# Order of the gate rows and of the residual tiles in the feed-forward stages of a two-layer encoder trunk

## The chip, the cores and the metric

The kernel runs on one core of a Trainium2 chip. The metric is the device time of one execution in microseconds; lower is better. The engines are TensorE (PE in the profile, its weight loads PEld), VectorE (DVE), ScalarE (ACT), GpSimd (POOL) and SyncE (SP, which here only issues transfers). Each engine works through its own queue in order, and they wait for each other by semaphores.

## The reference

Two layers over 512 frames of 1024 features, float32. Layer 0 has latent attention, layer 1 chunked attention with a relative-position bias; each is followed by a SwiGLU feed-forward with 2816 hidden features, and each sub-layer is wrapped in two RMS norms.

```
def swiglu(h, w_gate, w_up, w_down):
    return (jax.nn.silu(h @ w_gate) * (h @ w_up)) @ w_down

for layer in range(2):
    h = rms_norm(x, attn_pre_g[layer])
    ...
    x = x + rms_norm(y, attn_post_g[layer])
    h = rms_norm(x, ffn_pre_g[layer])
    f = swiglu(h, ffn_w_gate[layer], ffn_w_up[layer], ffn_w_down[layer])
    x = x + rms_norm(f, ffn_post_g[layer])
```

## The kernel before

All float32 products are done as three matmuls of a reduced type: each operand is split into a high half (a cast on ScalarE, `whi<-raw`, line 144) and a low half (a subtraction on VectorE, `wlo<-raw,whi`, line 146), and high-high, high-low and low-high are summed in PSUM. Three buffers each hold the halves of a weight tile, so the cast of a tile waits until the product three before it has been done.

The feed-forward hidden features come in blocks of 128. The first two blocks of a layer are done whole and kept in SBUF (`kept`, the tiles `fu`); the other 20 are done in ten pairs by `products`, pair 0 to 9, with a scheme of Strassen's kind: seven products (j = 0 to 6) of half size in place of eight. Each product is 24 matmuls of 128x256 on TensorE: two output halves e = 0, 1 of 12 each. The PSUM banks are `be` (products 0 and 6), `al` (1, 3, 4, 5) and `ga` (2). Product 5 adds to the banks that product 4 has filled, so the VectorE addition that reads product 4 out (`ut<-al,ut`, line 1648) must be done before product 5 starts in the same bank. In words like "fifth product", the product with j = 4 is meant. Sums of weight tiles are made partly by VectorE (`raw<-raw,raw`, line 202) and partly by transfers of GpSimd's queue that add in memory (line 185).

The gate rows: when the RMS norm's factor is known, it is spread over a tile `bc` (line 524), each finished gate block is multiplied by it (`fu<-fu,bc`, line 1236, for the two whole blocks, `gt<-gt,bc`, line 1594, for the others), goes through SiLU on ScalarE (line 1237 or 1595, the first with a load of the activation table) and is multiplied with its up block to a hidden tile `hd`, from which four half-size sums `hs` are formed for the down product. These are closures in the list `units`; `products` calls one at products 1, 3 and 5 of a pair (in pair 1 at product 6).

In layer 1 a generator `by_tokens` also runs beside the pairs from pair 2 on. For each of the eight residual tiles it loads 128x512 from the buffer `mid` in memory (`x<-mid`, line 1275, on SyncE), turns it in blocks of 32x32 on VectorE (`xt<-x`, line 1278) and stores it to the output in four transfers (`out_x<-xt`, line 1281), where the feed-forward result is added later. It is resumed at five of the seven products.

The order on each engine is set by a list scheduler over the traced program: what is ready first and stands first in the program is queued first. `with behind(ins):` queues the instructions of the block that are on the engine of `ins` behind `ins`, in the queue's order only, without a wait.

Of the kernel before, what the change touches and what calls it, by code (L numbers as in the profile page):

```python
# [14 lines left out]
OP = mybir.AluOpType  # L15
# [4 lines left out]
KT = D // P  # L20
# [48 lines left out]
def trunk(ctx: ExitStack, tc: tile.TileContext, a, out):  # L69
    nc = tc.nc  # L70
    V = nc.vector
# [20 lines left out]
    def bank(tag="mm", name="b"):  # L92
        return ps.tile([P, S], F32, tag=tag, name=name_(name), bufs={"mm": 4, "s": 2, "t": 2}[tag])
# [62 lines left out]
    class Pair:  # L156
# [35 lines left out]
        def load(self, j):  # L192

            if j == 0:
                self.raw[5] = self.tile(3)
            elif j in (1, 2):
                self.raw[j] = self.tile(j - 1)
                return self.last
# [78 lines left out]
    class Feed:  # L277
# [96 lines left out]
        def next(self, n, ahead=True):  # L374
            i = self.pos
            self.pos += 1
            assert self.plan[i][1] == n
            self.split(i + int(ahead))
            return self.ready[i]
# [44 lines left out]
    def behind(ins):  # L424

        return tc.issue_after(ins.ins) if ins is not None else nullcontext()

    def cut(t, c):
        return t[0][:, c], t[1][:, c]
# [412 lines left out]
    x = []  # L842
# [309 lines left out]
    def ffn(i, x_src, osp, firsts, late=()):  # L1152
# [96 lines left out]
        def step_():  # L1249
            for n in (5, 6):  # L1250
                with behind(at["ut"]), behind(feed.low):
                    feed.lows[base + n] = at["t"] = next(more)[1]
                if n == 5:
# [6 lines left out]
                    for k, (p, j) in enumerate([(0, 5), *((1, j) for j in range(7))]))  # L1260
        units = [lambda f=f: gate(*kept[2 * f:2 * f + 2]) for f in range(N_WHOLE)]
        products(xs, tb, rb, hid, side, units, empty, at, by_tokens(H) if i else None)
        post = (AfterLast if i else After)(i, eps, H)
        down(hid, post)
# [5 lines left out]

    def by_tokens(make):

        for k in range(KT):
            x = make(name="x")
            nc.sync.dma_start(x, a["mid"][:, k])
            yield
            t = make(name="xt")
            V.transpose(t, x)
            yield
            for q in range(4):  # L1280
                nc.sync.dma_start(
                    bass.AP(tensor=out.tensor, offset=out.offset + k * P + 32 * q, ap=[[D, 32], [32 * D, S // 32], [1, 32]]),
                    t[32 * q:32 * q + 32].rearrange("i (b j) -> i b j", j=32))
            yield
# [84 lines left out]
    A0, A1 = HALF  # L1369
# [216 lines left out]
    def products(xs, tb, rb, hid, side, units, empty, at, aside=None):  # L1586

        K2 = KT // 2
        moving = [[cut(tb[k][0], A0) for k in range(K2)], [cut(xs[k], A0) for k in range(K2)],
                  [cut(xs[k + K2], A0) for k in range(K2)], [cut(tb[k][0], A1) for k in range(K2)],  # L1590
                  [cut(tb[k][1], A0) for k in range(K2)], [cut(tb[k][1], A1) for k in range(K2)],
                  [cut(xs[k + K2], A1) for k in range(K2)]]
        def gated(t, u):
            V.tensor_tensor(t, t, rb[0], op=OP.mult)
            nc.scalar.activation(t, t, AF.Silu)
            h = hid.room()
            V.tensor_tensor(h, t, u, op=OP.mult)
            hid.add(h)

        pairs = (NF - N_WHOLE) // 2  # L1600
        done = mm = None
        for p in range(pairs):
            al, ga = [], []
            be = [bank("t" if p % 2 else "s", "be") for _ in range(2)]
            make = U if p > 3 else hid.make
            gate = [make(name="gt") for _ in range(2)]
            up_ = [make(name="ut") for _ in range(2)]
            for j in (range(7) if p else FIRST_TURN):
                if (p, j) in side:
                    side[p, j]()  # L1610
                if p and j in ((6,) if p == 1 else (1, 3, 5)[:2 + (aside is None or p % 2 == 0)]) and units:
                    units.pop(0)()
                if aside is not None and p > 1 and j in (0, 1, 3, 5, 6):
                    next(aside, None)
                w = feed.next(1024, 2)
                done = mm if p < 3 else None
                if p + 1 == pairs and j >= 4:
                    hid.ahead(j // 5)
                if j == 1:
                    al = [bank(name="al") for _ in range(2)]  # L1620
                if j == 2:
                    ga = [bank(name="ga") for _ in range(2)]
                to = (be, al, ga, al, al, al, be)[j]
                for e in range(2):
                    o = to[e][:, A0]
                    for k in range(K2):
                        l, r = w(e * S + k * P, P), moving[j][k]
                        first_ = j < 3 and k == 0
                        with behind(done):
                            for n, (c, d) in enumerate(((0, 0), (0, 1), (1, 0))):  # L1630
                                mm = nc.tensor.matmul(o, l[c], r[d], start=first_ and n == 0, stop=k == K2 - 1 and n == 2,  # L1631
                                                      skip_group_check=True)
                    t, u = gate[e], up_[e]
                    if j == 0:
                        at["ut"] = nc.scalar.copy(u[:, A1], o)
                    elif j == 1:
                        with behind(None if p else empty):
                            nc.scalar.copy(t[:, A0], o)
                    elif j == 2:
                        if p:  # L1640
                            V.tensor_tensor(t[:, A0], t[:, A0], o, op=OP.add)
                    elif j == 3:
                        nc.scalar.copy(t[:, A1], o)
                        if not p:
                            with behind(at["t"]):
                                V.tensor_tensor(t[:, A0], t[:, A0], ga[e][:, A0], op=OP.add)
                    elif j == 4:
                        V.tensor_tensor(u[:, A1], o, u[:, A1], op=OP.add)  # L1648
                    elif j == 5:
                        nc.scalar.copy(u[:, A0], o)  # L1650
                    else:
                        V.tensor_tensor(t[:, A1], t[:, A1], o, op=OP.add)
                        units.append(lambda t=t, u=u: gated(t, u))
                        while p > 6 and units:
                            units.pop(0)()
# [14 lines left out]
    x, sx = post.x, post.split  # L1670
# [21 lines left out]
    at = feed.pos  # L1692
# [249 lines left out]
```

## Time and profile before

| | |
|---|---|
| median of 3 runs | 1103.87 us (1102.91 to 1104.52) |
| profiled execution | 1103.36 us, of which the profile's span is 1101.6 us |
| granted TensorE clock, mean | 0.997 |
| busy: TensorE, VectorE, ScalarE, GpSimd | 99%, 83%, 63%, 12% of the span |
| matmuls of the ten pairs (line 1631) | layer 0: from 212.0 us on, layer 1: up to 985 us |

Rows of a timeline read: start in us, length in us, engine, line, operation, output and inputs by tile names, shape, count, and in brackets the idle time of the engine before it with what ended it. A row with x2 holds two instructions in a row. The ends of matmuls are modelled, so that their lengths overlap. In the chain of waits each row is a start, a length and what the time went to.

### The profile page before, as it was taken

How to read it: one execution, taken by the hardware profiler on the slowest of the kernel's cores; microseconds unless marked ns; L12 is line 12 of the kernel's file. 1: busy time of each engine (PE TensorE's matmuls, PEld its weight loads, DVE VectorE, ACT ScalarE, POOL GpSimd, SP SyncE). 2: the span in 40 equal slices, each digit the busy share in tenths (PEclk: the TensorE clock that was granted, in tenths of full speed). 3: DMA queues.
4: the chain of work that ended last, by engine and by line, in shares of the span. 5: the costliest groups of instructions: out<-in, count | busy, mean ns of one | idle time of the engine just before them, and what ended most of it. 6: DMA issues, size and time to landing. Idle time of an engine off the chain costs nothing.

```text
span 1101.6 us, 19401 instructions
## 1 busy us (share of the span) xinstructions
PE 1088.5 (99%) x7037; PEld 983.7 (89%) x7037; DVE 913.3 (83%) x1661; ACT 693.9 (63%) x1355; POOL 127.2 (12%) x193
## 2 busy tenths in 40 slices
PE   9999999999999999999999999999999999999997
PEld 7887889999999998888888888889999999998885
DVE  7787747889988879978858898758899989789977
ACT  7576637866555556668636767657765555566675
POOL 2211100111000001500000110000110010002401
PEclk9999999999999999999999999999999999999999
DMA  7444217797777648961555677618898888749913
GB/s 241 120 116 136 69 39 257 202 263 186 173 196 187 178 148 269 161 192 49 192 152 163 155 203 186 171 59 276 202 263 187 250 206 225 201 161 266 168 30 76
DMA packets 91216, 191.99 MB, mean 174 GB/s; under 512 B 27136, under 2 KB 28928, under 8 KB 91120
## 3 DMA queue, kind: packets, MB, share of 16 engines
q1 hardware_dynamic: 75904, 151.29, 44.2%
q0 software_dynamic: 14784, 39.02, 20.0%
q8 instruction: 55, 0.90, 0.3%
q10 hardware_dynamic: 432, 0.44, 0.1%
q14 instruction: 41, 0.34, 0.1%
HBM read 157.26 MB, written 10.88 MB: 153 GB/s over the span
## 4 chain that ended last, share of the span: by engine, by line
PE 96%; DMA 1%; DVE 1%; issue 1%; ACT 1%; SPq 0%; DVEq 0%; POOLq 0%; POOL 0%; ACTq 0%
PE al L1631 20%; PE b L393 10%; PE b L394 10%; PE b L395 10%; PE be L1631 10%; PE al L1362 8%; PE be L1362 5%; PE ga L1631 5%; PE de L1362 3%; PE ga L1362 3%; PE pt L577 2%; PE b L1792 2%; PE b L1125 1%; PE sc L1784 1%; DMA x<-mid 1%; PE sc L1783 1%
## 5 line engine op out<-in xcount | busy, mean ns | idle before, releaser
L144 ACT CAST whi<-raw 128x1024 fp32r<-128x1024 f32 (+3 forms) x224 | 225.1, 1006 | 189.6 <-PE al L1631 64.5
L146 DVE TENSOR_TENSOR wlo<-raw,whi 128x1024 fp32r<-128x1024 f32 (+3 forms) x224 | 260.9, 1167 | 58.2 <-ACT whi L144 56.6
L1631 PE MATMUL al<-th,whi 128*128 128x256 f32 x464 | 132.6, 286 | 2.0 <-DVE ut L1648 2.0
L1631 PE MATMUL al<-tl,whi 128*128 128x256 f32 x464 | 130.0, 280 | 0.0
L1631 PE MATMUL al<-th,wlo 128*128 128x256 f32 x464 | 130.0, 280 | 0.0
L1631 PEld LDWEIGHTS al<-th,whi 128*128 128x128 f32 x464 | 87.3, 188 | 4.6 <-DVE ut L1648 2.6
L1631 PEld LDWEIGHTS al<-tl,whi 128*128 128x128 f32 x464 | 87.4, 188 | 0.0
L1631 PEld LDWEIGHTS al<-th,wlo 128*128 128x128 f32 x464 | 87.3, 188 | 0.0
L564 ACT ACTIVATE p<-p,mn 128x128 f32<-128x128 f32 (+1 forms) x96 | 54.1, 563 | 35.2 <-DVE mn L562 33.2
L146 DVE TENSOR_TENSOR ptl<-pt,pth 128x128 fp32r<-128x128 f32 (+1 forms) x96 | 46.6, 486 | 31.2 <-ACT pth L144 30.4
L393 PE MATMUL b<-xh,whi 128*128 128x512 f32 x170 | 71.7, 422 | 0.0
L185 POOL DMA_DIRECT2D raw<-in_w_pair x40 | 35.4, 885 | 297.4 <-DMA raw<-in_w_pair 81.5
L146 DVE TENSOR_TENSOR wlo<-wd,whi 128x512 fp32r<-128x512 f32 x86 | 56.3, 685 | 14.6 <-ACT whi L144 14.4
L394 PE MATMUL b<-xl,whi 128*128 128x512 f32 x170 | 66.7, 393 | 0.0
L395 PE MATMUL b<-xh,wlo 128*128 128x512 f32 x170 | 66.7, 392 | 0.0
L144 ACT CAST whi<-wd 128x512 fp32r<-128x512 f32 x86 | 49.8, 619 | 24.0 <-PE al L1362 10.7
L144 ACT CAST pth<-pt 128x128 fp32r<-128x128 f32 (+1 forms) x96 | 40.3, 422 | 32.3 <-PE pt L577 31.4
L1362 PE MATMUL al<-whi,pl 128*128 128x512 f32 x132 | 51.4, 390 | 0.0
L1362 PE MATMUL al<-whi,ph 128*128 128x512 f32 x132 | 51.4, 389 | 0.0
L1362 PE MATMUL al<-wlo,ph 128*128 128x512 f32 x132 | 51.4, 389 | 0.0
L1631 PE MATMUL ga<-xh,whi 128*128 128x256 f32 x160 | 45.0, 281 | 0.0
L1631 PE MATMUL al<-xh,whi 128*128 128x256 f32 x160 | 44.9, 280 | 0.0
(332 smaller groups left out, 3482.6 us busy)
## 6 DMA issues: line engine op xcount, KB each, us to landing
raw<-in_w_pair SPq DMA_DIRECT2D x104, 512.0 KB, 5.3
raw<-in_w_pair POOLq DMA_DIRECT2D x40, 512.0 KB, 7.7
wd<-in_w_down SPq DMA_DIRECT2D x54, 256.0 KB, 5.4
raw<-in_w_o SPq DMA_DIRECT2D x16, 512.0 KB, 3.8
raw<-in_w_down SPq DMA_DIRECT2D x16, 512.0 KB, 3.9
raw<-in_w_qkb SPq DMA_DIRECT2D x16, 512.0 KB, 3.6
wd<-in_w_down POOLq DMA_DIRECT2D x22, 256.0 KB, 5.1
wd<-raw POOLq DMA_DIRECT2D x22, 256.0 KB, 4.2
```

What stands on the lines that cost most here:

```text
L144: hi = nc.scalar.copy(dst_hi, src)
L146: return hi, V.tensor_tensor(dst_lo, src, dst_hi.bitcast(F32), op=OP.subtract)
L185: return nc.gpsimd.dma_start(self.raw[j], src, accum_op=OP.add)
L393: nc.tensor.matmul(o, l[0], r[0], start=start, stop=False)
L394: nc.tensor.matmul(o, l[0], r[1], start=False, stop=False)
L395: last_mm[0] = nc.tensor.matmul(o, l[1], r[0], start=False, stop=stop)
L564: nc.scalar.activation(p[:, :n], p[:, :n], AF.Exp, bias=mn[:, :1], scale=-1.0, accum_out=self.sums[:, qt:qt + 1])
L577: nc.tensor.transpose(t[:, kt * P:(kt + 1) * P], p[:, kt * P:(kt + 1) * P], ident)
L1125: nc.tensor.matmul(o[:, q_], va[kt][:, part, v_], pt[:, kt, q_], start=n + kt == 0, stop=n == 2 and kt == NQT - 1)
L1362: nc.tensor.matmul(to[e], l[c], r[d], start=j < 4 and k == 0 and n == 0, stop=k == NF // 2 - 1 and n == 2, skip_group_check=True)
L1631: mm = nc.tensor.matmul(o, l[c], r[d], start=first_ and n == 0, stop=k == K2 - 1 and n == 2, skip_group_check=True)
L1792: nc.tensor.matmul(o[:, q_], vv, pt[:, kt, q_], start=pt is pth and kt == 0, stop=pt is ptl and kt == NQT - 1)
```

## The change

First, the units that are called in pairs 0 to 2 (in effect pairs 1 and 2) are queued on VectorE behind the last addition of a fifth product (`at["last"]`, which the fifth product now sets). Second, `by_tokens` issues the load of tile k + 1 at the step in which it used to issue only the load of tile k, so one more tile is held.

```
     def by_tokens(make):
 
-        for k in range(KT):
+        def load(k):
             x = make(name="x")
             nc.sync.dma_start(x, a["mid"][:, k])
+            return x
+
+        next_ = load(0)
+        yield
+        for k in range(KT):
+            x, next_ = next_, load(k + 1) if k + 1 < KT else None
             yield
             t = make(name="xt")
             V.transpose(t, x)
...
                 if p and j in ((6,) if p == 1 else (1, 3, 5)[:2 + (aside is None or p % 2 == 0)]) and units:
-                    units.pop(0)()
+                    with behind(at["last"] if p < 3 else None):
+                        units.pop(0)()
...
                     elif j == 4:
-                        V.tensor_tensor(u[:, A1], o, u[:, A1], op=OP.add)
+                        at["last"] = V.tensor_tensor(u[:, A1], o, u[:, A1], op=OP.add)
```

The number of instructions and their order on TensorE and GpSimd stay as they are. In the changed kernel the lines behind the first piece are 6 higher, and those behind the second 7, so `ut` is line 1655 there and `xt` line 1284.

VectorE in layer 0, from the end of pair 1's fourth product to pair 2's first (the numbers after the names tell tiles apart: `ut_2927` and `ut_2928` are the two additions of pair 1's fifth product, `wlo_3087` belongs to its seventh product, `wlo_3118` and `wlo_3159` to pair 2's first and second). Before:

```order
L202 TENSOR_TENSOR raw_2529<-raw_2529,raw_2776 128x1024
L1236 TENSOR_TENSOR fu_2639<-fu_2639,bc_3082 128x512
L1236 TENSOR_TENSOR fu_2641<-fu_2641,bc_3082 128x512
L146 TENSOR_TENSOR wlo_3087<-raw_2529,whi_3086 128x1024
L1648 TENSOR_TENSOR ut_2927<-al_2971,ut_2927 128x256
L1648 TENSOR_TENSOR ut_2928<-al_2972,ut_2928 128x256
L1239 SCALAR_TENSOR_TENSOR hd_3150<-fu_2639,fu_2640 128x512
L1594 TENSOR_TENSOR gt_2666<-gt_2666,bc_3082 128x512
L146 TENSOR_TENSOR wlo_3118<-raw_2887,whi_3117 128x1024
```

After:

```order
L202 TENSOR_TENSOR raw_2529<-raw_2529,raw_2776 128x1024
L1655 TENSOR_TENSOR ut_2927<-al_2971,ut_2927 128x256
L146 TENSOR_TENSOR wlo_3087<-raw_2529,whi_3086 128x1024
L1655 TENSOR_TENSOR ut_2928<-al_2972,ut_2928 128x256
L1236 TENSOR_TENSOR fu_2639<-fu_2639,bc_3082 128x512
L146 TENSOR_TENSOR wlo_3118<-raw_2887,whi_3117 128x1024
L1236 TENSOR_TENSOR fu_2641<-fu_2641,bc_3082 128x512
L202 TENSOR_TENSOR raw_2887<-raw_2887,raw_3010 128x1024
L1239 SCALAR_TENSOR_TENSOR hd_3150<-fu_2639,fu_2640 128x512
L1659 TENSOR_TENSOR gt_2925<-gt_2925,be_2923 128x256
L146 TENSOR_TENSOR wlo_3159<-raw_3010,whi_3158 128x1024
```

The two `fu` multiplications have moved from ahead of the `ut` additions to behind them, and the `gt` multiplications further back. Layer 1 has the same move at the same place.

ScalarE at the same place of layer 0. Before:

```order
L144 CAST whi_3086<-raw_2529 128x1024
L1237 ACT_TABLE_LOAD
L1237 ACTIVATE fu_2639<-fu_2639 128x512
L144 CAST whi_3117<-raw_2887 128x1024
L1237 ACTIVATE fu_2641<-fu_2641 128x512
L1650 COPY ut_2927<-al_2971 128x256
```

After:

```order
L144 CAST whi_3086<-raw_2529 128x1024
L144 CAST whi_3117<-raw_2887 128x1024
L1237 ACT_TABLE_LOAD
L1237 ACTIVATE fu_2639<-fu_2639 128x512
L1657 COPY ut_2927<-al_2971 128x256
L1657 COPY ut_2928<-al_2972 128x256
L144 CAST whi_3158<-raw_3010 128x1024
L1237 ACTIVATE fu_2641<-fu_2641 128x512
```

The cast for pair 2's first product has moved ahead of the table load and the first SiLU.

VectorE in layer 1 around the transposition of the last residual tile, which lies in pair 6 before the change (`ut_11095` is the first addition of that pair's fifth product in both). Before:

```order
L1641 TENSOR_TENSOR gt_11093<-gt_11093,ga_11182 128x256
L1278 STREAM_TRANSPOSE xt_11214<-x_11139 128x512
L1641 TENSOR_TENSOR gt_11094<-gt_11094,ga_11183 128x256
L1597 TENSOR_TENSOR hd_11281<-gt_10832,ut_10834 128x512
L146 TENSOR_TENSOR wlo_11219<-raw_10881,whi_11218 128x1024
L1327 TENSOR_TENSOR hs_11283<-hd_11212 128x256
L1328 SCALAR_TENSOR_TENSOR hs_11284<-hs_11283,hd_11281 128x256
L1329 TENSOR_TENSOR hs_11285<-hd_11281,hd_11212 128x256
L1330 SCALAR_TENSOR_TENSOR hs_11286<-hs_11284,hd_11281 128x256
L146 TENSOR_TENSOR wlo_11250<-raw_10793,whi_11249 128x1024
L1648 TENSOR_TENSOR ut_11095<-al_11148,ut_11095 128x256
```

After:

```order
L1648 TENSOR_TENSOR gt_11093<-gt_11093,ga_11182 128x256
L1334 SCALAR_TENSOR_TENSOR hs_11282<-hs_11281,hd_11279 128x256
L1648 TENSOR_TENSOR gt_11094<-gt_11094,ga_11183 128x256
L1335 TENSOR_TENSOR hs_11283<-hd_11279,hd_11212 128x256
L146 TENSOR_TENSOR wlo_11217<-raw_10881,whi_11216 128x1024
L1336 SCALAR_TENSOR_TENSOR hs_11284<-hs_11282,hd_11279 128x256
L1284 STREAM_TRANSPOSE xt_11289<-x_11053 128x512
L146 TENSOR_TENSOR wlo_11248<-raw_10791,whi_11247 128x1024
L1655 TENSOR_TENSOR ut_11095<-al_11148,ut_11095 128x256
```

The last `hd` and the first `hs` now stand ahead of this piece, the transposition of the last tile stands four places later, and its load was issued one step earlier.

## The prediction

> **What bounds the kernel now.** I read the page first, then the list of waits on TensorE, then the chain of waits, then the timelines of VectorE, ScalarE and TensorE around each wait that TensorE has in the two feed-forward stages. The page's first lines:
>
> ```profile
> span 1101.6 us, 19401 instructions
> PE 1088.5 (99%) x7037; PEld 983.7 (89%) x7037; DVE 913.3 (83%) x1661; ACT 693.9 (63%) x1355; POOL 127.2 (12%) x193
> ```
>
> TensorE is the bound nearly everywhere. An edit that leaves its instructions alone can only win what TensorE stands still, and that is little. The list of waits (engine, line, who was waited for, us in total, times, longest) has this row for the gate and up products:
>
> ```profile
> PE al L1631 <- DVE ut L1648: 2.0, 3, 0.7
> ```
>
> Three waits, all for `ut`, the addition that reads the fifth product (j = 4) out of PSUM; the sixth product (j = 5) writes the same banks and may not start before it. TensorE's timeline (start, us, operation, idle before) shows the three places:
>
> ```profile
> 247.00 0.28 PE L1631 MATMUL al<-th,wlo 128*128 128x256 f32 x1
> 247.91 0.39 PE L1631 MATMUL al<-th,whi 128*128 128x256 f32 x1 [0.62 <-DVE ut L1648]
> 248.14 0.28 PE L1631 MATMUL al<-tl,whi 128*128 128x256 f32 x1
> 248.26 0.28 PE L1631 MATMUL al<-th,wlo 128*128 128x256 f32 x1
> ...
> 821.50 0.39 PE L1631 MATMUL al<-th,whi 128*128 128x256 f32 x1 [0.66 <-DVE ut L1648]
> ...
> 921.98 0.38 PE L1631 MATMUL al<-th,whi 128*128 128x256 f32 x1 [0.67 <-DVE ut L1648]
> ```
>
> The first and second are in pair 1 of layers 0 and 1, the third in pair 6 of layer 1. A matmul here normally starts 0.12 us after the one before (248.14 to 248.26). The first wait has 0.91 us between two starts, so it costs 0.79, which is 0.17 more than its idle column says. After the restart the next matmul comes 0.23 later and not 0.12: another 0.11. With the same two additions the three places cost 0.90, 0.94 and 0.95 us, together 2.8 us. That is all there is to win, against 1101.6. The pace itself wanders a little from stretch to stretch without any wait, as two products of 24 matmuls in the chain of waits show:
>
> ```profile
> 356.71 2.82 PE al L1631 x24
> ...
> 376.74 2.85 PE al L1631 x24
> ```
>
> Why the idle column is too small: the reported end of a matmul lies 0.28 after its start, though the next one starts after 0.12. [...] By the idle column alone the sum would be 2.0 us and the forecast 1101.9; by the starts it is 2.8 us, which I take.
>
> **Why `ut` is late.** In layer 0, VectorE and then ScalarE:
>
> ```profile
> 243.40 1.22 DVE L202 TENSOR_TENSOR raw<-raw,raw 128x1024 f32<-128x1024 f32 x1
> 245.09 1.29 DVE L1236 TENSOR_TENSOR fu<-fu,bc 128x512 f32<-128x512 f32 x2 [0.47 <-ACT bc L524]
> 246.30 1.22 DVE L146 TENSOR_TENSOR wlo<-raw,whi 128x1024 fp32r<-128x1024 f32 x1
> 247.44 0.75 DVE L1648 TENSOR_TENSOR ut<-al,ut 128x256 f32<-128x256 f32 x2
> ...
> 244.95 1.05 ACT L144 CAST whi<-raw 128x1024 fp32r<-128x1024 f32 x1
> 246.02 1.28 ACT L1237 ACT_TABLE_LOAD   x1
> 247.31 0.63 ACT L1237 ACTIVATE fu<-fu 128x512 f32<-128x512 f32 x1
> 247.85 1.03 ACT L144 CAST whi<-raw 128x1024 fp32r<-128x1024 f32 x1
> ```
>
> VectorE stood 0.47 us for `bc`, then did two gate multiplications (1.29) and a weight split (1.22), and only then the two additions. The third place is another story. The chain of waits and VectorE's timeline, with one ScalarE row at the end:
>
> ```profile
> 906.47 9.75 DMA x<-mid
> 916.24 0.72 DVE xt L1278
> ...
> 915.07 0.42 DVE L1641 TENSOR_TENSOR gt<-gt,ga 128x256 f32<-128x256 f32 x1
> 916.24 0.71 DVE L1278 STREAM_TRANSPOSE xt<-x 128x512 f32<-128x512 f32 x1 [0.75 <-DMA x<-mid]
> 916.88 0.38 DVE L1641 TENSOR_TENSOR gt<-gt,ga 128x256 f32<-128x256 f32 x1
> 917.18 0.67 DVE L1597 TENSOR_TENSOR hd<-gt,ut 128x512 f32<-128x512 f32 x1
> 917.78 1.22 DVE L146 TENSOR_TENSOR wlo<-raw,whi 128x1024 fp32r<-128x1024 f32 x1
> ...
> 920.37 1.22 DVE L146 TENSOR_TENSOR wlo<-raw,whi 128x1024 fp32r<-128x1024 f32 x1
> 921.51 0.75 DVE L1648 TENSOR_TENSOR ut<-al,ut 128x256 f32<-128x256 f32 x2
> ...
> 918.27 1.05 ACT L144 CAST whi<-raw 128x1024 fp32r<-128x1024 f32 x1 [0.96 <-PE al L1631]
> ```
>
> The last of the eight residual tiles landed 9.75 us after its issue, VectorE stood 0.75 us for it, and all behind it in the queue, `ut` too, came that much later. All eight, by their line:
>
> ```profile
> L1275 SPq DMA_DIRECT2D x<-mid x8: 383/635/2710, 821.6 to 906.5; - x8
> ...
> DMA to landing us min/median/max: 3.2/5.6/9.7
> ```
>
> **The change, part by part.** No instruction is added or removed on any engine and TensorE's and GpSimd's order stays; only VectorE's, ScalarE's and SyncE's orders move. So the sum has two gains and the question of what is late next.
>
> *The gate rows (two places, layers 0 and 1).* I walk the new order by the durations above, on the clock of layer 0. A queued VectorE instruction starts some 0.08 us before the reported end of the one ahead (244.62 minus 243.40 is 1.22, and 246.30 comes 1.21 after 245.09 for two that report 1.29), so a split takes 1.14, an addition 0.34 and a multiplication 0.6 of the queue. Product 5 of pair 1 is 24 matmuls of 0.12 that end with the one at 247.00, so it starts at 244.2, and product 6 could start at 247.12. The first half of product 5 (12 matmuls of 0.12) is done at 245.9, and VectorE is free from 244.6: the first addition runs 245.9 to 246.3. It is due at 247.12, so 0.8 us early, where it is 0.7 late now. The split behind it (its cast ended at 246.00) ends at 247.5, the second addition at 247.9, due at 248.5, when product 6 reaches the other bank. The wait goes, and neither addition becomes a new one. Gain 0.90 and 0.94.
>
> What is late next there? ScalarE now does the cast for pair 2's first product ahead of the table load. That cast overwrites a buffer that product 5 reads (three buffers per weight half), so it starts at 247.3 and ends at 248.3; the table load follows to 249.6, the first SiLU to 250.2. VectorE's own work from 247.9 on (a multiplication, a split, a multiplication, a sum of two weight tiles: 0.6 + 1.14 + 0.6 + 1.14) lasts until 251.4, so `hd` finds its SiLU done; then `hd`, one addition and the split for pair 2's second product end at 253.5. That product is due at 255.6 (247.12 plus three products of 2.82). The margin is 2.1 us. The split for pair 2's first product ends at 249.7 against 252.8. Cost: nothing, covered by these margins. If the cover goes, each us beyond 2.1 costs one us per layer. The later gate rows (third and fourth multiplication, the SiLU behind them, `hd`, the four `hs`) feed only the down product, which begins after the tenth pair, eight pairs of seven products later; their delay of a few us is not waited for.
>
> *The residual tiles (third place).* A tile is now asked for one step ahead. Eight loads issued between 821.6 and 906.5 are 12.1 us apart, so the lead of the last one grows from 9.8 to about 22 us, against a slowest landing of 9.7. The 0.75 us goes. The new order also has the last `hd` ahead of this place and spreads the four `hs`, so I walk it too: product 6 would start at 921.15 (921.98 less 0.84), so product 3, three products of 2.82 earlier, was done at 915.7 and the second gate addition can start then, to 916.1; an `hs` to 916.4, the split behind the cast of 915.46 from 916.5 to 917.7, an `hs` and the transposition to 918.7, the next split after its cast (ended 919.3) to 920.5, `ut` to 920.9, against 921.15. Margin 0.2: enough, but the thinnest of all. Gain 0.95, bounded by 0 if another wait takes its place and by the whole 0.95.
>
> SyncE's queue: the loads stand one step earlier, the same 256 KB each, in front of one or two weight loads of 512 KB. One more tile of the ring stays occupied. TensorE's list of waits had no other row for these stages, so no weight was late, and I cost this at nothing; the bound is a loss of 3.2 us, the shortest landing of such a tile, if a weight that stands behind it had no slack at all.
>
> **The sum.** 0.90 + 0.94 + 0.95 = 2.8 us. The profiled execution took 1103.36; 1103.36 - 2.8 = 1100.6. The median of the three runs shown is 1103.87, 0.5 above it, so as a median 1101.1. That is 0.25% faster; 0.2% (2.2 us) is about what a measurement of this kernel can tell from no change. The sum sits close to that line, and 1% of matmul pace (2.82 against 2.85 is that much) over a tenth of the run is 1 us, so single runs scatter by about that (the three shown span 1.6 us).
>
> **The rivals.**
>
> *The third wait stays* (chance 0.12). Its margin is 0.2 us and the new order there differs in several rows; if the split ahead of `ut` or its cast comes 1 us later, the wait is back. Then only the gate rows count: 1.84 us, 1102.0 as a median. Against it: the two splits find their casts done, by the rows at 915.46 and 918.27.
>
> *Nothing is won* (0.07). The change would not do what it says if the scheduler's order left `ut` where it was; the order shows it moved. Or TensorE arrives 2.8 us earlier at a point that something else times, a transfer or the down stage's sums; the list of waits has no such row in those stages, so I give it little. 1103.9.
>
> *Slower* (0.05). In pair 2 of both layers the cast for its first product now stands in front of the table load on ScalarE. If that product's weight tile, which GpSimd's queue sums in memory, lands late, then the table load, the first SiLU, `hd` and in order behind them the split for the second product wait too; before, the load and SiLU were already done. It decides beyond the 2.1 us margin: the gain is lost at 3.5 us of delay, and at 5 us each layer loses 2.9, 5.8 together, minus 2.8: 1106.9. Against it: ScalarE did that cast in the trace right behind the SiLU, with no idle time for a transfer.
>
> **How the numbers follow.** All three waits go: 0.76, median 1101.1. With a scatter of about 0.7 us of a median, four in five of those cases are over 2.2 us, so 0.62 of the 0.76; the first rival adds 0.03: faster 0.65. The rest of these two and the case of nothing won: same 0.30. Slower 0.05. The range reaches down to 1099.9 (all gains and 1.2 us of pace) and up to 1103.0 (the first rival's 1102.0 and 1 us of pace).
>
> **What would show it.** In the changed kernel's list of waits the row of TensorE waiting for `ut` is gone or under 0.3 us; products 5 and 6 of pair 1 follow each other 0.12 us apart in both layers; VectorE has no idle time before a transposition; in pair 2, `hd` and the splits still end ahead of their products. Wrong would be a TensorE wait for a split, a cast or a copy in pairs 1 to 3, a stay of the wait in pair 6 of layer 1, or unchanged waits with a slower matmul pace.

## The result, and the profile after

| | before | after |
|---|---|---|
| median, same chip | 1103.87 us (7 runs, 1101.82 to 1104.52) | 1100.20 us (7 runs, 1099.20 to 1100.88) |
| profiled execution (span) | 1103.36 us (1101.6) | 1099.20 us (1097.4) |
| ratio of the times, 95% interval | | 0.9970 [0.9958, 0.9981] |

The change makes the kernel 0.3% faster. A second series of the same changed kernel beside other kernels gave 1100.86 us and 0.9972 [0.9960, 0.9983].

The first lines of the page of the changed kernel, and then its whole list of waits on TensorE:

```profile
span 1097.4 us, 19396 instructions
PE 1086.7 (99%) x7037; PEld 982.0 (89%) x7037; DVE 911.5 (83%) x1661; ACT 693.5 (63%) x1355; POOL 127.5 (12%) x193
...
PE sc L1112 <- ACT kh L144: 1.9, 1, 1.9
PE warm L113 <- DVE idle L110: 1.2, 1, 1.2
```

The row of TensorE waiting for `ut` is gone. Both rows that are left were there before and lie outside the feed-forward stages. Products are counted from one here, as in the prediction: products 5 and 6 are those with j = 4 and j = 5. TensorE's and VectorE's timelines at the first of the three places (pair 1 of layer 0):

```profile
245.74 0.28 PE L1638 MATMUL al<-th,wlo 128*128 128x256 f32 x1
245.86 0.28 PE L1638 MATMUL al<-th,whi 128*128 128x256 f32 x1
...
244.65 0.42 DVE L1655 TENSOR_TENSOR ut<-al,ut 128x256 f32<-128x256 f32 x1 [1.32 <-PE al L1638]
244.99 1.22 DVE L146 TENSOR_TENSOR wlo<-raw,whi 128x1024 fp32r<-128x1024 f32 x1
246.12 0.42 DVE L1655 TENSOR_TENSOR ut<-al,ut 128x256 f32<-128x256 f32 x1
246.46 0.68 DVE L1236 TENSOR_TENSOR fu<-fu,bc 128x512 f32<-128x512 f32 x1
```

The first addition now waits for TensorE and not TensorE for it: it ends at 245.07, product 6 starts at 245.86, 0.12 after the last matmul of product 5. At the third place (pair 6 of layer 1), and the eight loads by their line:

```profile
915.12 0.70 DVE L1284 STREAM_TRANSPOSE xt<-x 128x512 f32<-128x512 f32 x1
916.40 1.22 DVE L146 TENSOR_TENSOR wlo<-raw,whi 128x1024 fp32r<-128x1024 f32 x1 [0.58 <-ACT whi L144]
917.54 0.41 DVE L1655 TENSOR_TENSOR ut<-al,ut 128x256 f32<-128x256 f32 x1
...
918.10 0.28 PE L1638 MATMUL al<-th,wlo 128*128 128x256 f32 x1
918.22 0.28 PE L1638 MATMUL al<-th,whi 128*128 128x256 f32 x1
...
L1275 SPq DMA_DIRECT2D x<-mid x8: 383/446/2678, 819.2 to 893.2; - x8
...
DMA to landing us min/median/max: 4.2/4.9/7.6
```

The transposition has no idle time ahead of it: its tile was asked for at 893.2, 21.9 us earlier.

Since TensorE runs the same 7037 matmuls in the same order in both kernels, the start of each one after can be set against its start before, and the difference summed by stage:

| stage (us on the clock of before) | after minus before, us |
|---|---|
| 0 to 212, norms and attention of layer 0 | -1.22 |
| 212 to 413.5, pairs of layer 0 | -1.01, of it -0.91 at the wait in pair 1 |
| 413.5 to 785, down product of layer 0, attention of layer 1 | +0.04 |
| 785 to 988, pairs of layer 1 | -1.69, of it -0.92 and -0.93 at the two waits |
| 988 to the end, with the down product of layer 1 | +0.05 |

At the three waits TensorE gained 2.8 us. Another 1.2 us of this profile come from a stage that the change does not touch. There the windows of both profiles (us, busy time of each engine with its count, granted clock, DMA share, GB/s), first before, then after:

```profile
108.50:112.00 3.50, 3.50 (x14) 3.44 (x14) 3.36 (x9) 1.72 (x5) 0.40 (x1) 0.51 0.62 226
```

```profile
108.50:112.00 3.50, 3.50 (x22) 3.13 (x22) 3.36 (x9) 2.19 (x7) 0.52 (x1) 1.00 0.77 284
```

In the profiled execution of before, TensorE was granted half its clock (0.51) for these 3.5 us, and did 14 matmuls in place of 22; in that of after it was not. This stretch begins about 2 us after the wait `sc <- ACT kh`, which is 1.9 us long in both. It is a matter of the single execution (see the last section): the mean granted clock of the profiled execution of after is 0.999, that of the six other runs of after 0.996 or 0.997, about the 0.997 of before. So it is part of the difference of the two profiles, and nothing shows it in that of the medians.

### The profile page after: what moved, and what is told of

It reads as the page before. It is cut to its first block, busy times and chain, and to the rows that moved or that the text cites. A ratio compares the mean times of both kernels' runs of the same rounds, so it can differ in the third digit from the quotient of the medians.

```text
span 1097.4 us, 19396 instructions
## 1 busy us (share of the span) xinstructions
PE 1086.7 (99%) x7037; PEld 982.0 (89%) x7037; DVE 911.5 (83%) x1661; ACT 693.5 (63%) x1355; POOL 127.5 (12%) x193
## 4 chain that ended last, share of the span: by engine, by line
PE 98%; DVE 1%; ACT 0%; issue 0%; DMA 0%; DVEq 0%; POOLq 0%; POOL 0%; SPq 0%; ACTq 0%
PE al L1638 21%; PE b L393 10%; PE be L1638 10%; PE b L394 10%; PE b L395 10%; PE al L1368 8%; PE be L1368 5%; PE ga L1638 5%; PE de L1368 3%; PE ga L1368 3%; PE pt L577 2%; PE b L1799 2%; PE b L1125 1%; PE sc L1791 1%; PE sc L1790 1%; PE sc L1112 0%
## 5 line engine op out<-in xcount | busy, mean ns | idle before, releaser
L144 ACT CAST whi<-raw 128x1024 fp32r<-128x1024 f32 (+3 forms) x224 | 225.2, 1007 | 189.8 <-PE al L1638 60.3
L144 ACT CAST whi<-wd 128x512 fp32r<-128x512 f32 x86 | 49.8, 619 | 24.1 <-PE al L1368 10.7
L144 ACT CAST pth<-pt 128x128 fp32r<-128x128 f32 (+1 forms) x96 | 40.3, 422 | 32.2 <-PE pt L577 31.4
L1638 PE MATMUL al<-xl,whi 128*128 128x256 f32 x160 | 44.8, 280 | 0.0
```

Of the source, the lines that this page charges most:

```text
L144: hi = nc.scalar.copy(dst_hi, src)
```

## The experiments

They were measured in three groups, each beside runs of before: with a median of 1103.7 us in the first, 1103.49 in the second and 1103.16 in the third. Each kernel has one profile.

### The two parts alone

*Gate rows alone* (`by_tokens` as before):

```
+                    with behind(at["last"] if p < 3 else None):
+                        units.pop(0)()
...
+                        at["last"] = V.tensor_tensor(u[:, A1], o, u[:, A1], op=OP.add)
```

> Only the gate rows are queued behind the fifth product's additions; the residual loads stay as before. Theory (two separate causes): the waits of pair 1 in both layers go (0.90 and 0.94 us), the wait of pair 6 in layer 1 stays at about 0.95 us with VectorE idle before the last transposition, so about 1.8 us less than before, ratio 0.9983. Rival A (one cause: the new VectorE order of pairs 1 and 2 carries through to pair 6): all three waits go, 2.8 us less, 0.9975. Rival B (the gain comes from the matmul pace or the clock, not from the waits): TensorE's starts move apart from before outside the three places.

Measured: 1105.57 us, ratio 1.0012 [1.0002, 1.0022]. It is slower than before by 0.1%, and the expectation missed. Its list of waits on TensorE, the matmul that waits, VectorE, the piece of the chain of waits, and SyncE's queue:

```profile
PE al L1632 <- DVE wlo L146: 2.6, 1, 2.6
...
851.78 0.38 PE L1632 MATMUL al<-xh,wlo 128*128 128x256 f32 x1 [2.63 <-DVE wlo L146]
...
845.58 0.41 DVE L1330 SCALAR_TENSOR_TENSOR hs<-hs,hd 128x256 f32<-128x256 f32 x1
849.91 0.71 DVE L1278 STREAM_TRANSPOSE xt<-x 128x512 f32<-128x512 f32 x1 [3.91 <-DMA x<-mid]
850.54 1.18 DVE L146 TENSOR_TENSOR wlo<-raw,whi 128x1024 fp32r<-128x1024 f32 x1
...
841.29 8.60 DMA x<-mid
...
835.93 5.30 SPq L166 DMA_DIRECT2D raw<-in_w_pair  x2
841.29 0.42 SPq L1275 DMA_DIRECT2D x<-mid  x1
```

The waits for `ut` in pair 1 are gone, and so is the one in pair 6. But the load of the second residual tile now stands in SyncE's queue behind two weight loads that hold the queue for 5.30 us; it is issued at 841.29 and lands 8.60 us later. VectorE stands 3.91 us before the transposition, the split `wlo` of the next weight tile stands behind it, and TensorE waits 2.6 us for that. Before the change the same load was issued 4.5 us earlier, ahead of the weight loads, and VectorE did not stand (why the scheduler put the two weight loads first here, no run shows):

```profile
836.82 0.50 SPq L1275 DMA_DIRECT2D x<-mid  x1
837.43 5.07 SPq L166 DMA_DIRECT2D raw<-in_w_pair  x3
...
844.05 0.71 DVE L1278 STREAM_TRANSPOSE xt<-x 128x512 f32<-128x512 f32 x1
```

A second cost followed the wait. The windows around it:

```profile
849.00:852.36 3.36, 0.73 (x6) 0.58 (x5) 2.45 (x5) 1.20 (x2) 0.00 (x0) 1.00 1.06 274
852.36:855.77 3.41, 3.41 (x19) 3.41 (x18) 3.41 (x5) 0.63 (x1) 0.00 (x0) 0.51 0.77 130
855.77:860.00 4.23, 4.23 (x38) 4.23 (x37) 4.20 (x7) 3.16 (x5) 0.00 (x0) 1.00 0.64 190
```

From 0.58 us after the restart the granted clock is 0.51 for 3.41 us, in which matmuls start 0.213 us apart and not 0.1175: some 16 of them, so 1.5 us lost on top of the wait. By TensorE's starts, the stage from 785 to 988 us loses 3.27 us against before.

The wait of pair 6 is gone although nothing around it has moved. The last load and the transposition, from SyncE's and VectorE's timelines:

```profile
910.20 2.40 SPq L1275 DMA_DIRECT2D x<-mid  x1
...
918.82 0.41 DVE L1642 TENSOR_TENSOR gt<-gt,ga 128x256 f32<-128x256 f32 x1
919.33 0.71 DVE L1278 STREAM_TRANSPOSE xt<-x 128x512 f32<-128x512 f32 x1
```

VectorE's order from this `gt` to `ut` is that of before, and the load is issued 8.6 us ahead of the `gt`, as it is before (906.47 and 915.07). But the tile landed after 9.04 us and not after 9.75, so that VectorE stood 0.10 us for it and not 0.75. The third wait of before was thus the price of one slow landing; how often before has it cannot be told from its one profile.

*The load part alone* (the generator of the changed kernel, the units not queued):

```
+        def load(k):
...
+        next_ = load(0)
+        yield
+        for k in range(KT):
+            x, next_ = next_, load(k + 1) if k + 1 < KT else None
```

> Only the residual loads are issued one step ahead; the gate rows stay as before. Theory (two separate causes): both waits of pair 1 stay at 0.9 us each, the one of pair 6 goes, no VectorE idle time before a transposition, about 0.95 us less than before, ratio 0.9991, which the runs can hardly tell from the same. Rival A (one cause): nothing changes, the wait of pair 6 stays. Rival C (the late landing of the last load was chance in one profile): the wait of pair 6 is gone here, but it is gone in the run with the gate rows alone too.

Measured: 1102.50 us, ratio 0.9986 [0.9977, 0.9995]. The wait of pair 6 is gone, the two of pair 1 stay, as expected. But the sign of rival C is there too: that wait is also gone with the gate rows alone, so this run does not show that the earlier load is what removed it.

```profile
PE al L1637 <- DVE ut L1654: 1.3, 2, 0.7
```

So the parts do not add up: +1.3 us for the gate rows alone (0.0012 of 1103.7) and -1.5 us for the loads alone, but -3.3 us together (0.0030).

### What the gate rows need of the loads

*Only the second load early*, the gate rows moved as in the change:

```
-            x, next_ = next_, load(k + 1) if k + 1 < KT else None
+            x = early[k] if k < 2 else load(k)
```

where `early` holds the tiles of `load(0)` and `load(1)`, issued in the generator's first two steps.

> The gate rows moved, and of the loads of the residual only the second one (and the later transposition that goes with it) is issued early; the third and later ones are issued at their own step, as before. Theory (with the gate rows alone, the wait of 2.8 us in pair 2 of layer 1 comes from the second residual load, issued behind the third raw weight load): that wait of TensorE for `wlo` at 851 us is gone here, and the two waits for `ut` of pair 1 too, so the time is 1.8 to 2.8 us under the kernel before (ratio 0.9975 to 0.9985), and at least 3 us under the kernel with the gate rows alone. The third load now stands behind the raw loads instead; if it is late VectorE stands before the third transposition, near 862 us, and a wait of TensorE would show there. Rival (the wait came from the moved gate rows themselves, which fill VectorE and ScalarE in pair 2): it stays near 851 us, and the ratio is 1.000 to 1.002.

Measured: 1100.47 us, ratio 0.9968 [0.9957, 0.9979]. The loss of the gate rows alone is gone with this one load. Its row in SyncE's queue, and the kernel's list of waits on TensorE:

```profile
825.78 0.39 SPq L1275 DMA_DIRECT2D x<-mid  x1
...
PE sc L1112 <- ACT kh L144: 1.9, 1, 1.9
PE warm L113 <- DVE idle L110: 1.2, 1, 1.2
PE b L393 <- ACT whi L144: 0.2, 1, 0.2
```

It is issued 15.5 us earlier than in the kernel with the gate rows alone. The rival, that the moved gate rows themselves fill VectorE there, falls. The third transposition, at 859.27, did not wait for its load; VectorE stood once, for 1.1 us, before the sixth (`DMA x<-mid: 1.1, 1` in the transposition's group; issued at its own step at 883.92, landed 7.45 us later), and TensorE not at all. The wait in pair 6 is gone here too, although the last tile is loaded at its own step: it landed after 5.69 us, and the last `hd` and all four `hs` stand ahead of the transposition.

*Loads two steps ahead:*

```
+        held = [load(0), load(1)]
...
+            x = held.pop(0)
+            if k + 2 < KT:
+                held.append(load(k + 2))
```

> The changed kernel with the residual loads two steps ahead in place of one. Theory: one step is enough (lead 22 us against landings up to 9.7 us), nothing more is won and the extra load in front of the weights costs nothing: same as the changed kernel, 2.8 us less than before, 0.9975, no wait of TensorE for an addition. Rival E (loads that stand ahead of weights delay them): a new wait of TensorE or ScalarE for a weight in layer 1, some tenths of a us to 3 us slower than the changed kernel.

Measured: 1100.03 us, ratio 0.9967 [0.9955, 0.9980], the same as the changed kernel. One step is enough, and the residual loads in front of weight loads cost nothing measurable here.

*The units of pair 1 alone queued behind `ut`* (`p < 2` in place of `p < 3`):

> The changed kernel, but only the one unit called in pair 1 is queued behind the additions, those of pair 2 are free. Theory (what counts is what stands in VectorE's queue ahead of the additions; the order shows one fu and one gt multiplication of pair 2's units in the place that the first fu left): the waits of pair 1 stay in both layers at about 0.9 us each, only the load's 0.95 us is won, ratio 0.9991. Rival D (only the first unit is urgent, since it alone is called in pair 1): both waits of pair 1 go, 2.8 us, 0.9975.

Measured: 1102.51 us, ratio 0.9988 [0.9979, 0.9997]. The row of waits reads as in the kernel with the load part alone:

```profile
PE al L1638 <- DVE ut L1655: 1.3, 2, 0.7
```

When the unit called in pair 1 is moved, the scheduler puts the multiplications that are called in pair 2 into its place, ahead of `ut`. The bound on pair 2 is what makes the move work.

### The same queue, one step further

In the changed kernel one small thing is left in fifteen of the twenty pairs (2 to 9 of layer 0, 3 to 9 of layer 1). ScalarE, TensorE and VectorE in pair 2 of layer 0 (the copy of line 1650 reads the second half of product 4 out of the bank into which product 5 writes its second half):

```profile
262.88 1.05 ACT L144 CAST whi<-raw 128x1024 fp32r<-128x1024 f32 x1 [0.96 <-PE al L1638]
263.83 0.37 ACT L1650 COPY gt<-al 128x256 f32<-128x256 f32 x1
...
264.04 0.28 PE L1638 MATMUL al<-th,wlo 128*128 128x256 f32 x1
264.25 0.39 PE L1638 MATMUL al<-th,whi 128*128 128x256 f32 x1
264.48 0.28 PE L1638 MATMUL al<-tl,whi 128*128 128x256 f32 x1
```

The copy stands behind a cast and ends at 264.20. TensorE starts 0.21 us after the matmul before, then 0.23: 0.09 and 0.11 lost, 0.2 us a pair, too short for the list of waits. Three kernels, all on top of the changed one.

*Copy first*: the cast that follows is queued behind the copy.

```
+                if p and j == 4:
+                    feed.behind[len(feed.ready)] = (at["copy"],)
```

> The changed kernel, with ScalarE's cast for the seventh product's weights queued behind the second copy of the fourth product, so that this copy is no longer behind a cast. Theory: product 5's second half stops waiting for that copy, some 0.2 us in each of 20 pairs, up to 4 us in all, but the split that follows the cast moves back as well and VectorE's additions to `ut` come closer to being late: gain 0 to 2 us over the changed kernel (1098.2 to 1100.2). Rival (the cast behind the copy makes VectorE's split, and the `ut` additions behind it, late, so that product 6 waits): TensorE waits for `ut` come back in most pairs, and the time is 1 to 6 us above the changed kernel.

Measured: 1101.36 us, ratio 0.9980 [0.9971, 0.9989]: no gain, and by the median 0.5 us above the changed kernel of the same group. The stall at the copy is gone, but the split goes back with its cast and `ut` with the split, so that TensorE now steps at product 6. In pair 2 of layer 0:

```profile
266.67 0.39 PE L1640 MATMUL al<-th,whi 128*128 128x256 f32 x1 [0.19 <-DVE ut L1657]
...
265.06 1.23 DVE L146 TENSOR_TENSOR wlo<-raw,whi 128x1024 fp32r<-128x1024 f32 x1 [1.18 <-ACT whi L144]
266.20 0.74 DVE L1657 TENSOR_TENSOR ut<-al,ut 128x256 f32<-128x256 f32 x2
```

The same step, 0.20 to 0.47 us between two starts and 0.22 or 0.23 to the next, stands at the start of product 6 in all fifteen pairs, mostly too short for the list of waits. In fourteen of them two to six matmuls of product 7 run ahead of it, so here the order on TensorE is not quite that of before.

*`ut` first*: the first addition to `ut` goes ahead of that split, the copy stays.

```
-                w = feed.next(1024, 2)
+                w = feed.next(1024, 1 if p and j == 4 else 2)
...
+                        if p and not e:
+                            feed.lows[len(feed.ready)] = at["last"]
+                            feed.ahead(1)
```

> One half of the fastest kernel so far: VectorE's first addition to `ut` is queued ahead of the split that stood before it, but ScalarE's second copy of the fourth product stays behind the cast. Theory (the 0.2 us of a pair at product 5 are waits for that copy): they stay, and moving the `ut` addition alone wins nothing, 1099.5 to 1101, ratio 0.996 to 0.998. Rival (the gain came from the earlier `ut` addition alone): 1096 to 1098, ratio 0.993 to 0.995.

Measured: 1100.53 us, ratio 0.9974 [0.9964, 0.9984]: nothing won by the time; the 0.2 us per pair at the copy stay in its trace (0.09 and 0.11 at each of the eight pairs from 255 to 413 us).

*Copy and `ut` first*: both edits.

```
+                            feed.behind[len(feed.ready)] = (at["copy"],)
+                            feed.lows[len(feed.ready)] = at["last"]
+                            feed.ahead(1)
```

> As the kernel with the copy first, and VectorE's first addition to `ut` is also queued ahead of the split that stood before it. Theory: both small waits of a pair go, the copy's of some 0.2 us and none for `ut` in its place: 2 to 4 us under the changed kernel (1096.2 to 1098.2). Rival (the split that now stands behind the addition comes late for product 7, or the small steps between products 4 and 5 are not waits for the copy but pace): no gain, 1099.5 to 1101, or TensorE waits for `wlo` at product 7 and the time is above the changed kernel.

Measured: 1096.28 us, ratio 0.9932 [0.9919, 0.9944], the fastest kernel of the study and 4.6 us under the changed kernel of the same group (1100.86). The same place:

```profile
262.98 0.37 ACT L1650 COPY gt<-al 128x256 f32<-128x256 f32 x1 [1.03 <-PE al L1638]
263.25 1.05 ACT L144 CAST whi<-raw 128x1024 fp32r<-128x1024 f32 x1
...
264.07 0.28 PE L1638 MATMUL al<-th,wlo 128*128 128x256 f32 x1
264.19 0.28 PE L1638 MATMUL al<-th,whi 128*128 128x256 f32 x1
...
264.39 0.42 DVE L1655 TENSOR_TENSOR ut<-al,ut 128x256 f32<-128x256 f32 x1 [1.25 <-PE al L1638]
264.73 1.22 DVE L146 TENSOR_TENSOR wlo<-raw,whi 128x1024 fp32r<-128x1024 f32 x1
```

The copy is done at 263.35, TensorE passes the bank without a step, and from 255 to 409 us, where the pairs end, no two starts are more than 0.13 us apart. Each of the two edits alone won nothing in the time; together they take the stall away. In the profiles, layer 0's stage gains 2.3 us on the changed kernel and layer 1's only 0.3, although the 0.2 us per pair are gone there too: all along layer 1's pairs matmuls start 118.7 ns apart, where the changed kernel has 117.3 in half of the stretches (see the last section). Summed over the starts, the steps taken away are worth 1.9 us in layer 0 and 1.4 in layer 1; the pace gave another 0.5 in layer 0 and took 1.1 back in layer 1.

*Key split first*, on top of the last kernel: `with first(40): split(kh, kl, bk)` in the attention of layer 0, aimed at the wait near 107 us.

> The kernel with copy and `ut` first, and the split of the key tile ahead of other work in the attention before the feed-forward, where TensorE stands 1.9 us near 107 us in every profile and half of the profiles show a half-clock stretch right behind it. Theory: the wait shrinks by up to 1.9 us, no half-clock stretch of 3.4 us follows it, and the time is 0.5 to 2 us under that kernel with a narrower scatter (1094.3 to 1095.8). Rival (what stands ahead of the split is needed as early, so that another wait takes its place): 1095.8 to 1098, and a wait of 1 to 3 us for another tile in the same place.

Measured: 1098.00 us, ratio 0.9953 [0.9940, 0.9965]. The wait did not move (`PE sc L1113 <- ACT kh L144: 1.9, 1, 1.9`), and the kernel is 1.7 us slower by the medians. The edit did not reach the place that it was aimed at: against copy and `ut` first, the order of instructions differs only between 61 and 74 us, and near 107 us the order of ScalarE's casts is the same. So whether an earlier split would shorten the wait was not tested. By TensorE's starts its two feed-forward stages are the same as those of copy and `ut` first (-3.42 and -1.98 us against before, there -3.35 and -1.97); the whole difference of the two profiles, 1.96 us, lies ahead of 212 us. Of it 0.6 is there at 60 us, ahead of the first instruction that moved, 0.7 at 107 us and 1.9 at 112.5 us: the last step is the stretch at half clock, which this profile has and the faster one has not (0.79 against 1.00 in the table below). In the timed runs the mean granted clock does not tell the two kernels apart, 0.997 in all five here and in four of five there, so what the 1.7 us of the medians are stays open.

### All kernels by stage

The same sum of TensorE's starts against before, for every profiled execution. The first column of numbers is the pairs of both layers, which the edits touch, the second the stage ahead of them with the wait near 107 us.

| kernel | both feed-forward stages, us | 0 to 212, us | clock 106 to 114 | ratio |
|---|---|---|---|---|
| before | 0 | 0 | 0.79 | 1 |
| gate rows alone | +2.17 | +1.08 | 0.79 | 1.0012 |
| load part alone | -0.81 | +0.56 | 0.79 | 0.9986 |
| pair 1 alone | -1.18 | +1.19 | 0.79 | 0.9988 |
| copy first | -1.80 | -0.38 | 0.79 | 0.9980 |
| changed kernel | -2.70 | -1.22 | 1.00 | 0.9970 |
| changed kernel, second series | -2.58 | -0.61 | 1.00 | 0.9972 |
| two steps ahead | -2.45 | -0.53 | 1.00 | 0.9967 |
| second load early | -2.92 | -0.50 | 1.00 | 0.9968 |
| `ut` first | -4.11 | +0.69 | 0.79 | 0.9974 |
| copy and `ut` first | -5.32 | -1.20 | 1.00 | 0.9932 |
| key split first | -5.40 | +0.76 | 0.79 | 0.9953 |

The seven profiles with the slow stretch have a mean of +0.56 us in the stage ahead, the five without -0.81: it is worth some 1.4 us of a profile. Directly, by TensorE's starts, after is 0.13 us later than before at 107 us and 1.24 earlier at 115. `ut` first stands 1.4 us below the changed kernel in the feed-forward stages although its steps at the copy are all there; 1.1 of it is pace (117.3 and 117.4 ns from start to start as means of the two layers, against 117.6 and 117.7), and the time shows no gain.

## Why the prediction was right, and where not

The forecast was 1101.1 us with a range of 1099.9 to 1103.0; measured were 1100.2.

- *The places and their price.* All three waits went. Predicted were 0.90, 0.94 and 0.95, in all 2.8 us; the starts right before and behind them moved together by 0.91, 0.92 and 0.93, 2.8 us. The idle column alone, 2.0 us, would have been too little, so the reading by starts held.
- *The walk through the new order.* Pair 1: the first addition was to be 0.8 us early; it ends 0.79 us ahead of product 6. Pair 6: the margin was to be 0.2 us, and `ut` ends at 917.95, 0.27 us ahead of 918.22. In pair 2 of layer 0, the split for the second product was to be 2.1 us early; it ended at 252.10, and that product starts at 254.3, 2.2 us later.
- *The step that failed: the parts as separate terms.* The sum took 1.84 us for the gate rows and 0.95 for the loads, and the rival "the third wait stays" counted on 1102.0 with the gate rows alone. Measured alone, the gate rows lose 1.3 us, and no wait of pair 6 is in it. The walk of the gate rows looked at VectorE and ScalarE and not at SyncE's queue, where the second residual load slid behind two weight loads. The load part, costed as 0.95 us, is what keeps the gate rows from costing; beside them it is worth 0.0042 (1.0012 to 0.9970), 4.6 us. The prediction asked what the loads do to the weights behind them, which is nothing; the danger was the other way round. That the sum came right although its terms were not independent is luck: both parts happened to be in one change.
- *The third price.* The forecast put the wait of pair 6 down to the landing of 9.75 us and asked for the tile earlier. The mechanism is right: in the changed kernel the tile is there 17.7 us before its transposition. But the 0.95 us are the price of that one landing. With the gate rows alone, order and lead are those of before, the tile landed after 9.04 us, and the wait is gone; in the twelve profiles the last load took 3.8 to 9.75 us. So it is partly luck that a full 0.95 belongs in the sum.
- *The size.* The medians fell by 3.67 us in the first series and by 2.63 in the second, against 2.8 forecast; the first series' interval of 0.9958 to 0.9981 is 2.1 to 4.6 us, so the runs do not tell any of these from 2.8. The two profiles differ by 4.2 us, of which 1.2 are the half-clock stretch near 110 us. The prediction read the waits and not the granted clock, and put the scatter down to the pace of matmuls alone.
- *The rivals.* "The third wait stays" and "nothing is won" did not come. "Slower" was put on ScalarE's cast in front of the table load; that cast ran at 245.98 and the load behind it at 247.05, with the SiLU done at 248.97 and `hd` starting at 249.94, so it was not late. A slower ending was a live one, but by the residual load in SyncE's queue.

## What to carry to other kernels

When a few instructions are put behind others by hand, every queue that the scheduler then fills differently must be walked, the DMA queue with them: here the edit that removes two waits makes a kernel slower until a load in another queue is moved as well. The two parts of this change, which meet in SyncE's queue, had no prices of their own (+1.3 and -1.5 us alone, -3.3 together); measure each alone and together. The stalls of 0.09 and 0.11 us did not show in the list of waits, but in the distance between starts, and fifteen pairs with two of them each, taken away by two edits that each won nothing in the time alone, were worth about as much (3.3 us by the starts, 2.6 in the two stages, where the pace took some back) as the three waits that the list did show. A difference of 1 us between two profiles can be the clock or the pace of one execution (here some 1.4 and 1.1 us): look at the granted clock of the other runs before putting it down to an edit.

## What the runs showed of the hardware

Some waits of TensorE of 1.9 to 2.6 us were followed by 3.41 us at half clock, which cost another 1.4 to 1.5 us. In the kernel with the gate rows alone, the wait of 2.6 us that ends at 851.78 was followed from 852.36 on by 3.41 us at a granted clock of 0.51; the wait of 1.9 us near 107 us had such a stretch behind it in seven of the twelve profiles (0.79 in the table above) and in five it had not (1.00). In the profile of before the record of the granted clock begins at 6.11 us and changes at 108.51, 111.92 and 1098.37. The stretch at half clock is 3.413 us long, and the three changes lie 30, 31 and 320 times that behind the start of the record. In the profile of after the record begins at 6.64 and the only change, at 1095.49, lies 319 times that behind it. Laid out from the start of the record in stretches of this length, those with the wait near 107 us read, first of before, then of after:

```profile
105.10:108.51 3.41, 1.84 (x12) 1.63 (x13) 3.32 (x5) 2.49 (x6) 0.81 (x3) 1.00 0.75 200
```

```profile
102.21:105.62 3.41, 2.67 (x16) 1.97 (x14) 2.21 (x7) 3.32 (x8) 0.75 (x1) 1.00 0.45 108
105.62:109.04 3.42, 2.24 (x15) 2.01 (x15) 3.42 (x6) 2.10 (x5) 1.05 (x2) 1.00 0.75 207
```

In before, 1.57 of the 1.92 us lie in one such stretch, which has 1.84 us of matmuls, and the next one is at half clock. In after the wait is split, 0.74 and 1.18 us, and the clock stays at 1.00. That this split decides it is not shown: near the end of after, a stretch with 1.52 us of matmuls (1088.66 to 1092.08) was followed by one at a clock of 1.00. What brings the half clock about is open; no run was made for it.

In these profiles the pace of matmuls does not wander, it holds one of a few values. Taken in stretches of 20 us (mean distance of starts under 0.13 us, in ns), the pairs of each layer read:

| kernel | layer 0, 260 to 400 us | layer 1, 840 to 980 us |
|---|---|---|
| before | 117.8 118.1 117.8 117.3 117.3 118.3 117.8 | 117.3 118.7 117.3 117.3 117.3 118.6 117.4 |
| changed kernel | 117.3 117.3 118.4 117.6 117.3 118.4 117.6 | 118.5 117.4 117.3 117.6 118.5 117.3 117.4 |
| two steps ahead | 118.7 118.6 118.7 118.7 118.7 117.7 117.3 | 117.5 118.5 117.3 117.3 117.3 117.3 117.4 |
| copy and `ut` first | 117.3 117.3 117.3 117.3 117.3 117.3 117.3 | 118.7 118.7 118.7 118.7 118.7 118.7 118.6 |

It is 117.3 or 118.7, the values between are stretches in which it switches, and without a stall (the last row) it keeps one for a whole layer; the key split first repeats that row. A stall does not have to change it: `ut` first, with the steps in every one of these pairs, keeps 117.3 through the same stretch of layer 0. Nor are there only two: with pair 1 alone, matmuls start 120.0 ns apart from 825 to 860 us. Over the 1687 starts of a layer's pairs the difference between the two usual values is some 2.3 us. What sets it is open; no run was made for it.
